# A low-rank update on one core: x's column blocks taken with a step of six, and A and B loaded behind the first piece of x

## The chip, the cores and the metric

The kernel runs on one core of one Trainium2 chip. A time is the device time of one execution in microseconds (us). Beside it stand the numbers of one profiled execution: its span runs from the first to the last instruction that the hardware profiler recorded, and some time lies around it. TensorE is PE in the profile (PEld is its weight load, which can run beside a matmul), VectorE is DVE, ScalarE is ACT, GpSimd is POOL, SyncE is SP. A small q behind a name (SPq, ACTq) is that engine's instruction sequencer, which also issues DMAs.

## What is computed

```python
batch, seq, d_model, r = 16, 512, 768, 16
# x [16, 512, 768] float32, A [768, 16], B [16, 768], scale 0.5
lora = np.matmul(np.matmul(x, A), B)
return (x + scale * lora).astype(np.float32)
```

With the first two axes of x flattened there are 8192 rows (tokens) of 768 float32. x is 25.17 MB, the output is as large, and A and B are 48 KB each.

## The kernel before

**Loads and stores.** The 8192 tokens are cut into six parts, `PARTS = [2, 6, 8, 16, 16, 16]`, in units of 128 tokens. Part i is loaded by one DMA into a tile of 128 partitions by S rows of 768 float32, S being its entry in the list; partition p gets S neighbouring tokens, so each partition's piece is one contiguous run of S times 3072 bytes. All x loads and all stores are issued by SyncE and so share one DMA queue (q1 in the profile) in the order in which they are issued: the loads of parts 0 to 4 (line 68), the load of part 5 (line 96), and then the stores (line 155) as parts are finished. Parts 0 to 3 are each stored in one DMA, parts 4 and 5 in two halves of eight rows (3.1 MB each). The result is written over x in place (line 145), so a part needs no second buffer.

**A and B.** TensorE multiplies over the partitions, so A's 768 rows must come to lie as six blocks of 128 partitions. Column block j of x is its columns 128j to 128j+127, and block j of A is the rows with these numbers. A row of A is only 16 float32, or 64 bytes. So A is loaded as 24 runs of 2048 bytes, 32 rows of A each (line 79, issued by ScalarE on its own queue, q10), into a corner of the room that part 5 will take later. GpSimd has cleared that corner first (line 78). VectorE then transposes it in blocks of 32 by 32 (line 87) and four casts (line 91) put the result into `a_mm`, float16, [128, 6, 16]. B is loaded by ScalarE as well (line 80) and cast to float16 (line 93). Because part 5's tile is the same memory as this corner, its load waits until VectorE has read A and B from there.

**The work on x.** The 64 row blocks are handled in 17 chunks of up to four. For each chunk:
- `transposed`: for each of six column blocks j, TensorE transposes the chunk's 128x128 float32 blocks into PSUM (line 113; up to four transposes), and ScalarE copies the result to SBUF as float16 (line 115). In a transpose the block of x is the stationary operand, loaded by LDWEIGHTS, and the identity matrix moves past it.
- `projected`: six matmuls, one for each j, add up (x A) transposed, 16 by 512 (line 122); VectorE multiplies by the scale and casts (line 127).
- `added`: for each 128 tokens two matmuls of 512 and 256 columns with B (line 139), and VectorE adds the result to x (line 145).
- `finished`: issues a store when its last chunk is added (line 155).

**Order.** The loop at the end of the kernel interleaves the chunks: half of chunk c's transposes, half of chunk c-1's `added`, the rest of the transposes, the rest of `added`, then `projected`. The framework's scheduler may move an instruction when its own estimate of the times says that another can go first, and it did so around the first parts. Each engine then works through its own instructions in order; semaphores carry the dependences.

Of the kernel before, what the change touches and what calls it, by code (L numbers as in the profile page):

```python
# [1 line left out]

# [6 lines left out]


MM_DT = mybir.dt.float16

PARTS = [2, 6, 8, 16, 16, 16]

STORES = {4: [8, 8], 5: [8, 8]}

CHUNK = 4


@with_exitstack  # L20
def kernel(
    ctx: ExitStack,
    tc: tile.TileContext,
    x: bass.AP,
    A: bass.AP,
    B: bass.AP,
    scale: bass.AP,
    out: bass.AP,
):

    nc = tc.nc
    fp32 = mybir.dt.float32
    P = 128

    x2 = x.flatten_outer_dims()
    out2 = out.flatten_outer_dims()
    T, D = x2.shape
    R = A.shape[1]  # L40
    ND = D // P
    assert D % P == 0 and sum(PARTS) * P == T
    n_splits = [(n0, min(512, D - n0)) for n0 in range(0, D, 512)]
    sc = float(scale)

    const = ctx.enter_context(tc.tile_pool(name="const", bufs=1))
    xpool = ctx.enter_context(tc.tile_pool(name="xp", bufs=1))
    xtpool = ctx.enter_context(tc.tile_pool(name="xtp", bufs=6))
    ypool = ctx.enter_context(tc.tile_pool(name="yp", bufs=2))
    ps_xt = ctx.enter_context(tc.tile_pool(name="ps_xt", bufs=3, space=bass.MemoryType.PSUM))  # L50
    ps_y = ctx.enter_context(tc.tile_pool(name="ps_y", bufs=1, space=bass.MemoryType.PSUM))
    ps_l = ctx.enter_context(tc.tile_pool(name="ps_l", bufs=2, space=bass.MemoryType.PSUM))


    parts = []
    tok = 0
    for i, S in enumerate(PARTS):
        parts.append([None, tok, S])
        tok += S * P

    def rows(t2, i):
        _, tok0, S = parts[i]
        return t2[ds(tok0, S * P), :].rearrange("(p s) d -> p s d", s=S)

    def loaded(i):
        S = parts[i][2]
        parts[i][0] = xpool.tile([P, S, D], fp32, name=f"x_sb{i}")
        nc.sync.dma_start(out=parts[i][0], in_=rows(x2, i))  # L68


    last = len(parts) - 1
    lastpool = ctx.enter_context(tc.tile_pool(name="lastp", bufs=1))
    room = lastpool.tile([P, parts[last][2], D], fp32, name="room", tag="last")
    NB = D // 32
    a_rows = room[0:32, 0, 0 : 32 * R].rearrange("b (a r) -> b a r", r=R)
    a_t = room[0:32, 1, 0 : 32 * R].rearrange("a (r b) -> a r b", r=R)
    b_f32 = room[0:R, 2, :]
    nc.gpsimd.memset(a_rows, 0.0)  # L78
    nc.scalar.dma_start(out=a_rows[0:NB, :, :], in_=A.rearrange("(b a) r -> b a r", a=32))
    nc.scalar.dma_start(out=b_f32, in_=B)  # L80
    loaded(0)
    loaded(1)
    for i in range(2, last):
        loaded(i)


    nc.vector.transpose(out=a_t, in_=a_rows.rearrange("b a r -> b r a"))  # L87
    a_mm = const.tile([P, ND, R], MM_DT, name="a_mm")
    a_tv = a_t[:, :, 0:NB].rearrange("a r (c k) -> a k c r", k=4)
    for k in range(4):  # L90
        nc.vector.tensor_copy(out=a_mm[ds(32 * k, 32), :, :], in_=a_tv[:, k, :, :])  # L91
    b_mm = const.tile([R, D], MM_DT, name="b_mm")
    nc.vector.tensor_copy(out=b_mm, in_=b_f32)  # L93

    parts[last][0] = lastpool.tile([P, parts[last][2], D], fp32, name="x_last", tag="last")
    nc.sync.dma_start(out=parts[last][0], in_=rows(x2, last))

    ident = const.tile([P, P], fp32, name="ident")
    make_identity(nc, ident)


    chunks = [
        (i, s0, min(CHUNK, S - s0))
        for i, (_, _, S) in enumerate(parts)
        for s0 in range(0, S, CHUNK)
    ]
    state = {}

    def transposed(c, j):
        i, s0, n = chunks[c]  # L110
        xt_ps = ps_xt.tile([P, CHUNK, P], fp32, name="xt_ps")
        for s in range(n):
            nc.tensor.transpose(xt_ps[:, s, :], parts[i][0][:, s0 + s, ds(j * P, P)], ident)  # L113
        xt_sb = xtpool.tile([P, CHUNK * P], MM_DT, name="xt_sb")
        nc.scalar.copy(out=xt_sb[:, 0 : n * P], in_=xt_ps[:, 0:n, :])  # L115
        state[c, j] = xt_sb

    def projected(c):
        n = chunks[c][2] * P
        ps_yt = ps_y.tile([R, CHUNK * P], fp32, name="ps_yt")  # L120
        for j in range(ND):
            nc.tensor.matmul(  # L122
                ps_yt[:, 0:n], a_mm[:, j, :], state.pop((c, j))[:, 0:n],
                start=(j == 0), stop=(j == ND - 1),
            )
        yt_sb = ypool.tile([R, CHUNK * P], MM_DT, name="yt_sb")
        nc.vector.tensor_scalar(  # L127
            out=yt_sb[:, 0:n], in0=ps_yt[:, 0:n], scalar1=sc, scalar2=None,
            op0=mybir.AluOpType.mult,
        )  # L130
        state[c] = yt_sb

    def added(c, subs):
        i, s0, n = chunks[c]
        subs = [s for s in subs if s < n]
        lora = {s: ps_l.tile([P, D], fp32, name="lora_ps") for s in subs}
        for s in subs:
            for n0, w in n_splits:
                nc.tensor.matmul(  # L139
                    lora[s][:, ds(n0, w)], state[c][:, ds(s * P, P)], b_mm[:, ds(n0, w)],  # L140
                    start=True, stop=True,
                )
        for s in subs:
            xs = parts[i][0][:, s0 + s, :]
            nc.vector.tensor_tensor(out=xs, in0=xs, in1=lora[s], op=mybir.AluOpType.add)  # L145

    def finished(c):
        i, s0, n = chunks[c]
        del state[c]
        end = 0  # L150
        for w in STORES.get(i, [parts[i][2]]):
            end += w
            if end == s0 + n:
                piece = slice(end - w, end)
                nc.sync.dma_start(out=rows(out2, i)[:, piece, :], in_=parts[i][0][:, piece, :])

    for c in range(len(chunks)):
        for j in range(3):
            transposed(c, j)
        if c >= 1:  # L160
            added(c - 1, (0, 1))
        for j in range(3, ND):
            transposed(c, j)
        if c >= 1:
            added(c - 1, (2, 3))
            finished(c - 1)
        projected(c)
    c = len(chunks) - 1
    added(c, (0, 1))
    added(c, (2, 3))  # L170
    finished(c)


# [1 line left out]
_INS = ['x', 'A', 'B', 'scale']  # L175
_OUTS = [((16, 512, 768), 'float32')]

_NUMBERS = {'scale': 0.5}


# [26 lines left out]
```

## Time and profile before

| | |
|---|---|
| time, median of 3 runs | 124.87 us (124.79 to 125.25) |
| the profiled execution: its own time | 124.9 us |
| the profiled execution: its span | 123.1 us |
| PE busy (matmuls and transposes) | 97.8 us, 79% |
| DVE busy | 70.3 us, 57% |
| ACT busy | 52.5 us, 43% |
| bytes moved by DMA | 50.54 MB, mean 410 GB/s over the span |
| first x load issued, landed | 0.74 us, 6.1 us |
| second x load landed; PE's next transpose | 11.6 us; 11.76 us |
| last x load landed | 64.1 us |
| last store issued, landed | 110.46 us, 122.3 us |

Busy time counts an engine's own instructions. Idle time on an engine that is not the bound costs nothing, and a busy share near 80% does not make an engine the bound: what matters is which wait ends last. The windows of the profile give, for a stretch of the span, each engine's busy time, the granted TensorE clock, the share of the 16 DMA engines' time that is filled with packets, and the rate.

### The profile page before, as it was taken

To read this page: it belongs to the slowest core of one execution; us is meant where nothing else is said; L and a number is where in the kernel's file an instruction comes from. 1 tells how busy PE (TensorE), PEld (TensorE's weight loads), DVE (VectorE), ACT (ScalarE), POOL (GpSimd) and SP (SyncE) were. 2 spreads that over 40 slices of the span, in tenths; PEclk is the share of its full clock that TensorE was granted. 3 is DMA by queue.
4 is the path that set the end of the run, shared out by engine and by line. 5 is a ranking of instruction groups with operands and counts; after the bars stand their busy time and mean duration, and the time that the engine had idled before them with its cause. 6 is when DMAs were issued, how large, how long until landed. Compare 5 with 4: busy or idle time off the path is not lost.

```text
span 123.1 us, 1615 instructions
## 1 busy us (share of the span) xinstructions
PE 97.8 (79%) x614; PEld 60.8 (49%) x614; DVE 70.3 (57%) x87; ACT 52.5 (43%) x103; POOL 1.1 (1%) x7
## 2 busy tenths in 40 slices
PE   0095999999949999999999999999999999530000
PEld 0083765657328566656657474757565666100000
DVE  0261056755884276868686868685767768880000
ACT  3060556455406573645555564737373736000000
POOL 3000000000000000000000000000000000000000
PEclk9999999999999999999999999999999999995555
DMA  2999998999799699799799999989979999999981
GB/s 61 406 431 427 471 519 367 415 500 431 335 511 479 290 511 468 319 479 495 295 411 462 444 407 495 479 351 479 452 311 463 415 439 426 421 447 439 415 383 64
DMA packets 2092, 50.54 MB, mean 410 GB/s; under 512 B 252, under 2 KB 252, under 8 KB 548
## 3 DMA queue, kind: packets, MB, share of 16 engines
q1 hardware_dynamic: 2016, 50.33, 95.6%
q10 hardware_dynamic: 68, 0.10, 0.4%
q8 instruction: 5, 0.08, 0.3%
q14 instruction: 3, 0.02, 0.0%
HBM read 25.26 MB, written 25.17 MB: 410 GB/s over the span
## 4 chain that ended last, share of the span: by engine, by line
PE 71%; DMA 8%; DVE 7%; issue 1%; DVEq 1%; SPq 0%; ACT 0%; ACTq 0%
PE xt_ps L113 38%; PE lora_ps L139 18%; PE ps_yt L122 15%; DMA x_sb<-in_x_dram 8%; DVE x_last L145 3%; DVE x_sb L145 3%; DVE yt_sb L127 1%; DVEq L202 1%; SPq L68 0%; ACT xt_sb L115 0%; ACTq L115 0%
## 5 line engine op out<-in xcount | busy, mean ns | idle before, releaser
L115 ACT CAST xt_sb<-xt_ps 128x512 f16<-128x512 f32 (+1 forms) x102 | 51.2, 569 | 49.9 <-PE xt_ps L113 49.6
L145 DVE TENSOR_TENSOR x_sb<-x_sb,lora_ps 128x768 f32<-128x768 f32 x48 | 43.5, 950 | 21.2 <-PE lora_ps L139 21.2
L113 PE MATMUL xt_ps<-ident,x_sb 128*128 128x128 f32 x288 | 39.7, 290 | 7.7 <-DMA x_sb<-in_x_dram 7.6
L113 PEld LDWEIGHTS xt_ps<-ident,x_sb 128*128 128x128 f32 x288 | 33.1, 147 | 16.7 <-issue 11.5
L139 PE MATMUL lora_ps<-b_mm,yt_sb 16*128 16x512 f16 (+1 forms) x128 | 26.8, 324 | 3.8 <-DVE yt_sb L127 1.6
L122 PE MATMUL ps_yt<-xt_sb,a_mm 128*16 128x512 f16 (+1 forms) x102 | 24.4, 375 | 0.0
L145 DVE TENSOR_TENSOR x_last<-x_last,lora_ps 128x768 f32<-128x768 f32 x16 | 14.5, 950 | 5.3 <-PE lora_ps L139 5.3
L139 PEld LDWEIGHTS <-yt_sb 16*128 16x128 f16 x128 | 9.5, 92 | 15.3 <-issue 8.3
L127 DVE TENSOR_SCALAR yt_sb<-ps_yt 16x512 f16<-16x512 f32 (+1 forms) x17 | 10.9, 642 | 7.9 <-PE ps_yt L122 7.9
L122 PEld LDWEIGHTS <-a_mm 128*16 128x16 f16 x102 | 7.9, 91 | 13.0 <-issue 5.1
L113 PE MATMUL xt_ps<-ident,x_last 128*128 128x128 f32 x96 | 12.2, 277 | 0.0
L113 PEld LDWEIGHTS xt_ps<-ident,x_last 128*128 128x128 f32 x96 | 10.3, 140 | 3.0 <-PE ps_yt L122 1.7
L93 DVE CAST b_mm<-room 16x768 f16<-16x768 f32 x1 | 0.5, 548 | 4.4 <-DMA room<-in_B_dram 4.4
L115 ACT ACT_TABLE_LOAD x1 | 1.3, 1283 | 1.9 <-POOL ident masks.py:199 1.9
L87 DVE STREAM_TRANSPOSE room<-room 32x512 f32<-32x512 f32 x1 | 1.0, 1031 | 1.1 <-DMA room<-in_A_dram 1.1
L91 DVE CAST a_mm<-room 32x96 f16<-32x96 f32 x4 | 0.9, 232 | 0.1
L78 POOL MEMSET room<- 32x512 f32 x1 | 0.5, 515 | 0.3 <-POOLq L188 0.3
masks.py:199 POOL TENSOR_SCALAR_AFFINE_SELECT ident<-ident 128x128 f32<-128x128 f32 x1 | 0.3, 292 | 0.1
masks.py:197 POOL MEMSET ident<- 128x128 f32 x1 | 0.2, 194 | 0.0
L188 POOL MEMSET const-bfloat16-1.0<- 128x1 bf16 x1 | 0.1, 101 | 0.0
L188 POOL MEMSET const-uint8-127<- 128x1 uint8 x1 | 0.1, 101 | 0.0
L188 POOL MEMSET const-float32-0.0<- 128x1 f32 x1 | 0.1, 98 | 0.2 <-issue 0.2
(1 smaller groups left out, 0.1 us busy)
## 6 DMA issues: line engine op xcount, KB each, us to landing
x_sb<-in_x_dram SPq DMA_DIRECT2D x2, 6144.0 KB, 39.7
out_dram<-x_sb SPq DMA_DIRECT2D x3, 3072.0 KB, 21.6
x_last<-in_x_dram SPq DMA_DIRECT2D x1, 6144.0 KB, 56.0
out_dram<-x_sb SPq DMA_DIRECT2D x1, 6144.0 KB, 28.2
out_dram<-x_last SPq DMA_DIRECT2D x2, 3072.0 KB, 13.5
x_sb<-in_x_dram SPq DMA_DIRECT2D x1, 3072.0 KB, 17.3
x_sb<-in_x_dram SPq DMA_DIRECT2D x1, 2304.0 KB, 10.5
out_dram<-x_sb SPq DMA_DIRECT2D x1, 2304.0 KB, 44.6
```

What stands on the lines that cost most here:

```text
L78: nc.gpsimd.memset(a_rows, 0.0)
L87: nc.vector.transpose(out=a_t, in_=a_rows.rearrange("b a r -> b r a"))
L91: nc.vector.tensor_copy(out=a_mm[ds(32 * k, 32), :, :], in_=a_tv[:, k, :, :])
L93: nc.vector.tensor_copy(out=b_mm, in_=b_f32)
L113: nc.tensor.transpose(xt_ps[:, s, :], parts[i][0][:, s0 + s, ds(j * P, P)], ident)
L115: nc.scalar.copy(out=xt_sb[:, 0 : n * P], in_=xt_ps[:, 0:n, :])
L122: nc.tensor.matmul(ps_yt[:, 0:n], a_mm[:, j, :], state.pop((c, j))[:, 0:n], start=(j == 0), stop=(j == ND - 1),)
L127: nc.vector.tensor_scalar(out=yt_sb[:, 0:n], in0=ps_yt[:, 0:n], scalar1=sc, scalar2=None, op0=mybir.AluOpType.mult,)
L139: nc.tensor.matmul(lora[s][:, ds(n0, w)], state[c][:, ds(s * P, P)], b_mm[:, ds(n0, w)], start=True, stop=True,)
L145: nc.vector.tensor_tensor(out=xs, in0=xs, in1=lora[s], op=mybir.AluOpType.add)
L188: nc = _bacc.Bacc("TRN2", target_bir_lowering=False, num_devices=1)
L202: with _tile.TileContext(nc) as tc:
```

## The change

A's rows are split the other way: partition k gets the six rows 6k to 6k+5, which are one contiguous run of 384 bytes, so A is one plain load of 128 such runs into `a_f32` and one cast to `a_mm`. The clearing, the 32x32 transpose and three of the four casts are gone. For the product to stay the same, column block j of x becomes the columns j, j+6, j+12, ...: a transpose now reads 128 float32 that lie 24 bytes apart in each partition, where before it read 128 neighbouring ones. The sum over the six blocks covers all 768 columns either way.

A and B are issued by SyncE, on x's queue, directly behind the load of part 0 and ahead of the load of part 1. They have tiles of their own, so part 5 takes an ordinary tile and its load is issued right behind that of part 4, with no wait.

```diff
-    last = len(parts) - 1
-    lastpool = ctx.enter_context(tc.tile_pool(name="lastp", bufs=1))
-    room = lastpool.tile([P, parts[last][2], D], fp32, name="room", tag="last")
-    NB = D // 32
-    a_rows = room[0:32, 0, 0 : 32 * R].rearrange("b (a r) -> b a r", r=R)
-    a_t = room[0:32, 1, 0 : 32 * R].rearrange("a (r b) -> a r b", r=R)
-    b_f32 = room[0:R, 2, :]
-    nc.gpsimd.memset(a_rows, 0.0)
-    nc.scalar.dma_start(out=a_rows[0:NB, :, :], in_=A.rearrange("(b a) r -> b a r", a=32))
-    nc.scalar.dma_start(out=b_f32, in_=B)
+    a_f32 = const.tile([P, ND, R], fp32, name="a_f32")
+    b_f32 = ypool.tile([R, D], fp32, name="b_f32", bufs=1)
     loaded(0)
-    loaded(1)
-    for i in range(2, last):
+    nc.sync.dma_start(out=a_f32, in_=A.rearrange("(k j) r -> k j r", j=ND))
+    nc.sync.dma_start(out=b_f32, in_=B)
+    for i in range(1, len(parts)):
         loaded(i)
-    nc.vector.transpose(out=a_t, in_=a_rows.rearrange("b a r -> b r a"))
     a_mm = const.tile([P, ND, R], MM_DT, name="a_mm")
-    a_tv = a_t[:, :, 0:NB].rearrange("a r (c k) -> a k c r", k=4)
-    for k in range(4):
-        nc.vector.tensor_copy(out=a_mm[ds(32 * k, 32), :, :], in_=a_tv[:, k, :, :])
+    nc.vector.tensor_copy(out=a_mm, in_=a_f32)
     b_mm = const.tile([R, D], MM_DT, name="b_mm")
     nc.vector.tensor_copy(out=b_mm, in_=b_f32)
-    parts[last][0] = lastpool.tile([P, parts[last][2], D], fp32, name="x_last", tag="last")
-    nc.sync.dma_start(out=parts[last][0], in_=rows(x2, last))
...
+    def xt_in(i, s, j):
+        return parts[i][0][:, s, :].rearrange("p (k j) -> p j k", j=ND)[:, j, :]
...
-            nc.tensor.transpose(xt_ps[:, s, :], parts[i][0][:, s0 + s, ds(j * P, P)], ident)
+            nc.tensor.transpose(xt_ps[:, s, :], xt_in(i, s0 + s, j), ident)
```

## The prediction

> **What bounds the kernel now.** I first read the page's table of 40 slices and its queue list.
>
> ```profile
> PE   0095999999949999999999999999999999530000
> PEclk9999999999999999999999999999999999995555
> DMA  2999998999799699799799999989979999999981
> ...
> q1 hardware_dynamic: 2016, 50.33, 95.6%
> q10 hardware_dynamic: 68, 0.10, 0.4%
> ```
>
> Two rows are dense: PE stops near slice 36, the DMA engines go on to the end. The windows settle which one ends last; the columns are the stretch, busy time and count of each engine, granted clock, share of the 16 DMA engines, GB/s.
>
> ```profile
> 1.80:2.40 0.60, 0.00 (x0) 0.00 (x0) 0.00 (x0) 0.55 (x1) 0.00 (x0) 1.00 0.78 169
> 2.40:3.00 0.60, 0.00 (x0) 0.00 (x0) 0.00 (x0) 0.60 (x1) 0.00 (x0) 1.00 0.57 102
> 3.00:64.10 61.10, 54.54 (x338) 34.64 (x339) 35.68 (x47) 29.43 (x61) 0.00 (x0) 1.00 1.00 428
> 64.10:110.46 46.36, 43.25 (x278) 26.19 (x276) 34.63 (x42) 21.89 (x42) 0.00 (x0) 1.00 1.01 431
> 110.46:112.80 2.34, 0.00 (x0) 0.00 (x0) 0.00 (x0) 0.00 (x0) 0.00 (x0) 0.50 1.05 452
> 112.80:119.50 6.70, 0.00 (x0) 0.00 (x0) 0.00 (x0) 0.00 (x0) 0.00 (x0) 0.50 1.00 429
> 119.50:122.30 2.80, 0.00 (x0) 0.00 (x0) 0.00 (x0) 0.00 (x0) 0.00 (x0) 0.50 0.23 97
> ```
>
> From 3.0 to 119.5 us the DMA engines are full, at about 430 GB/s. The kernel is bound by its 50 MB; computing only has to hand over each store before the queue is empty. The tightest place is the last store, issued at 110.46. The three last rows move 1.06 + 2.87 + 0.27 = 4.2 MB after that; the store itself is 3.15 MB, so 1.05 MB is still ahead of it: 2.45 us at 430 GB/s. A store issued into an empty queue would start about 1.1 us after its issue (the first load: issued at 0.74, first bytes at about 1.8). So **PE and what follows it may be 2.45 - 1.1 = 1.35 us later at no cost**; beyond that each us costs about one. This cover is small, because PE never rests: the chain of waits runs through PE from the landing of part 1 to the end.
>
> ```profile
> 11.76 2.79 PE xt_ps L113 x12
> ...
> 40.23 1.39 PE ps_yt L122 x6
> 41.62 1.46 PE xt_ps L113 x12
> 43.08 0.75 PE lora_ps L139 x4
> 43.83 1.46 PE xt_ps L113 x12
> ```
>
> No DMA wait stands in it after 11.76, so whatever makes a transpose slower accumulates from there.
>
> **The transposes, the part with the largest possible price.** 384 of them now load a stationary block whose elements lie 24 bytes apart. What a load has to spare is in narrow stretches of the timeline and in the groups by shape (start or busy us, mean ns).
>
> ```profile
> 70.62 0.20 PEld L113 LDWEIGHTS xt_ps<-ident,x_sb 128*128 128x128 f32 x2 [0.43 <-PE ps_yt L122]
> ```
> ```profile
> 70.78 0.25 PEld L113 LDWEIGHTS xt_ps<-ident,x_sb 128*128 128x128 f32 x2
> ```
> ```profile
> L113 PEld LDWEIGHTS xt_ps<-ident,x_last 128*128 128x128 f32 x96 | 10.3, 140 | 3.0 <-PE ps_yt L122 1.7 <-issue 1.3
> L122 PEld LDWEIGHTS <-a_mm 128*16 128x16 f16 x102 | 7.9, 91 | 13.0 <-issue 5.1
> L91 DVE CAST a_mm<-room 32x96 f16<-32x96 f32 x4 | 0.9, 232 | 0.1
> ```
>
> One load record is 140 ns. The first two of a run of twelve together take 200, so the second starts 60 ns after the first: a load reads its 128 columns in about 60 ns. (The record of a load of 16 columns is 91 ns; 112 columns more make 49, which agrees.) Later pairs take 250, so they start 110 ns apart: inside a run the pace is set by the transposing matmul, and the load lies under it with about 50 ns to spare. The first load of a run has no cover; between the runs PE changes to other matmuls.
>
> No row shows PE reading with a step, so I bound the new load from both sides. Below: 60 ns, nothing changes (less is excluded, as the same 128 columns are read). Above: the cast into a_mm reads on VectorE, each of its 96 elements 128 bytes from the last. The scale-and-cast takes 409 ns for 256 columns and 673 for 512, so 1.03 ns each and 145 fixed; 96 at that pace make 244, and the cast took 232. So a step costs VectorE nothing, and a new place in every 1.03 ns is reached. If PE could do no better, a load would take 128 x 1.03 + 5 = 137 ns. Between 60 and 137 I take the middle, about 100: neither row is PE with a step. That is still under the 110. Then only the first load of each run shows: two runs for each of 16 chunks after part 1's landing, 32 x 40 ns = **1.3 us**, just the cover of 1.35. At 137 ns: 32 x 77 = 2.5 us, and the 340 others pass the cover by 27 ns, 9.2 us; together 11.7.
>
> [...]
>
> **A, B and the queue.** The profile gives A and B's queue (q10) 0.4% of 16 engines' span: 0.49 us of every engine. Afterwards there are 128 + 16 pieces in place of 24 + 16. Below: by bytes alone 98 KB at 430 GB/s is 0.23 us, a gain of 0.26. Above: if a piece of A's takes as long as q10's average packet (0.49 x 16 / 68 = 0.115 us), 144 x 0.115 / 16 = 1.04 us, a loss of 0.55. I take 0.5, no change, since bytes fall short of a small piece's fixed part and the average packet is far larger than 384 bytes.
>
> [...]
>
> At the start, 1.8 to 3.0 us moved 101 + 61 = 163 KB where the full rate makes 514: 0.8 us lost, while part 0 and B share the engines. With B behind part 0, between nothing and 0.8 comes back. I take 0.1, because a queue that starts up alone also has to fill. On SyncE two issues, 0.54 and 0.41 us as ScalarE's took, now stand ahead of part 1's: it is issued at about 2.1 instead of 1.17 and could start at 3.2. Part 0's 0.79 MB last until 1.8 + 1.8 = 3.6, so it is not late. If that cover were gone it would cost the difference, as PE waits for part 1. Part 5's load, issued at 8.17 now, comes earlier behind 19 MB of queue, which hides its issue time either way: it lands at 64.1 and PE needs it at about 80. The stores are issued from 17 us on, and no wait is added.
>
> **What goes from the prologue**: the 0.52 us clearing on GpSimd, the 1.03 us transpose and three casts of 0.23 on VectorE. a_mm is now ready at 8.1 us and first used at 8.97, behind chunk 0's transposes; afterwards A lands soon after part 0. PE then waits for part 1 until 11.76 anyway, idle 1.34 us, so these gains go into that wait. If A came later than now, the same 1.34 us would hide it.
>
> **Sum**, from this execution's span of 123.1 and 1.8 us around it (124.9; the median is 124.87): transposes +1.3, less 1.35 of cover, and about 0.3 because the 16 engines do not come free at one moment and some would wait; A and B 0; start -0.1. That is +0.2: **125.1 us**, with 124.3 to 125.5 as this case's own range.
>
> **Rivals.**
> - *The load overtakes its cover* (slower). Place: line 113's pace. Price: above about 100 to 110 ns the cover is used up, and from 110 on each further ns costs 372 ns in all. At 115 ns: 32 x 55 + 340 x 5 = 3.5 us, less 1.35: 127.0. At 137: 11.7 less 1.35: 135.3. For it: every element is at a new place, and cover and middle value are near each other. Against: the cast on VectorE. The lower half is likelier, since PE's own load of neighbouring columns reads twice as fast as VectorE.
> - *Several times longer* (slower). A load of 230 ns, about four times: 32 x 170 + 340 x 120 = 46 us, less 1.35: near 170. Nothing in the trace excludes it, the cast's row speaks against it.
> - *Faster by over 0.5%.* The load stays near 60 ns, and the start gives back most of its 0.8 with A's pieces cheap (-0.26): 123.8 to 124.2. For it: the slow 1.2 us at the start. Against: the bytes are the same and 116 of 123 us are full.
> - *The short pieces do not pay*: A's pieces at the upper bound, +0.55, with the load hidden: 125.4 to 125.6. I count it in the forecast's edge.
>
> **How the numbers follow.** Forecast 46%; load overtakes 32%, two thirds of that below 131; several times longer 12%; faster 10%. 0.5% is 0.62 us, about what a measurement of this kernel can tell from no change. Faster by more: 0.10. Within: 0.45, the forecast less its upper edge and a little of the first rival. Slower: 0.45. The range runs from 124.0 into the first rival up to 131.0; beyond it lie the rest of that rival and the second.
>
> **What will show it.** Right: loads of line 113 recorded at about 180 instead of 140 ns; transposes still 110 ns apart; twelve in about 1.5 us; the last store issued near 111.8; DMA full to about 119.5. Wrong: a run of twelve well over 1.5 us, a last store issued after 112, empty DMA slices ahead of it; or loads still at 140 and the start fuller, then the gain of the third rival. An early order of PE's work changed by the scheduler would move the last store too, by an amount that this trace cannot give.

## The result, and the profile after

The changed kernel takes 133.76 us (median of 6 runs) against 124.88 before; the ratio is 1.0697, with a 95% interval of 1.0666 to 1.0728. (One of the six runs, of 135.2 us, fell into a slower state of the chip and is left out of the ratio.) The forecast of 125.1 us was wrong, and so was the range up to 131.0: the first rival came true near its upper end. The profiled execution took 133.08 us with a span of 131.3, 8.2 us longer than before.

The same rows of the page as before:

```profile
PE   0384999999769999999999999999999999973000
PEclk9997699999995999999999999999999999999555
DMA  4999999999999999998999999998999922890885
...
q1 hardware_dynamic: 2192, 50.43, 90.7%
```

PE is still dense up to slice 36 or 37, of a longer span now. What is new stands in the DMA row: slices 33 and 34 hold a 2, and slice 37 a 0. Windows of the changed kernel (stretch, busy time of each engine, granted clock, DMA share, GB/s) show these holes in us:

```profile
64.90:105.00 40.10, 40.10 (x236) 27.55 (x236) 25.70 (x31) 20.50 (x37) 0.00 (x0) 1.00 1.01 432
105.00:111.60 6.60, 6.60 (x41) 4.51 (x40) 4.23 (x5) 3.41 (x7) 0.00 (x0) 1.00 0.28 119
111.60:118.50 6.90, 6.11 (x35) 3.51 (x34) 4.52 (x6) 2.93 (x6) 0.00 (x0) 1.00 0.95 400
118.50:122.60 4.10, 0.96 (x4) 0.27 (x3) 3.25 (x4) 0.00 (x0) 0.00 (x0) 0.80 0.02 4
122.60:130.50 7.90, 0.00 (x0) 0.00 (x0) 0.00 (x0) 0.00 (x0) 0.00 (x0) 0.50 0.93 398
```

Up to 105 us the queue is full, as before. Then it runs dry twice, because the last two stores are not issued yet. PE, busy without a gap up to 116.9 us, has become the bound of the last 25 us; the last store is issued at 121.78 us, 11.3 later than before. The chain of waits shows where PE's time went (start, us, what):

```profile
44.88 1.82 PE xt_ps L101 x12
46.70 0.75 PE lora_ps L127 x4
47.45 1.83 PE xt_ps L101 x12
49.28 0.75 PE lora_ps L127 x4
50.03 1.39 PE ps_yt L110 x6
```

The matmuls with A and B take 1.39 and 0.75 us as before. Only a run of twelve transposes is longer, 1.82 where it was 1.46. A chunk has two, so it takes 6.54 us in place of 5.81; 16 chunks of 0.73 make 11.7, and 11.3 were measured. That the two are so near is partly luck. From the fourth store to the last both kernels run at the full granted clock, and the seven chunks whose transposes lie there lose 5.13 us, 0.73 each, as they should. Between the third store and the fourth, four chunks lose 4.65 us in place of 2.9; there the granted clock stood at half from 39.1 to 42.5 us in this execution, and not in that of the kernel before. Up to the third store only 1.54 us are lost.

Inside a run, in narrow stretches of the timeline of the weight loads (start, busy us), and over all loads (mean ns):

```profile
70.99 0.35 PEld L101 LDWEIGHTS xt_ps<-ident,x_sb 128*128 128x128 f32 x2 [0.43 <-PE ps_yt L110]
```
```profile
71.23 0.38 PEld L101 LDWEIGHTS xt_ps<-ident,x_sb 128*128 128x128 f32 x2
```
```profile
L101 PEld LDWEIGHTS xt_ps<-ident,x_sb 128*128 128x128 f32 x384 | 57.5, 236 | 18.3 <-issue 8.1 <-PE ps_yt L110 5.6 <-ACT xt_sb L103 4.6
L79 DVE CAST a_mm<-a_f 128x96 f16<-128x96 f32 x1 | 0.2, 211 | 5.3 <-DMA a_f<-in_A_dram 5.3
```

A record is about 240 ns now. The first two loads of a run cover 350, so the second starts 110 ns after the first (60 before; single records say 107 and 57). Two later ones cover 380, so they start 140 ns apart (110 before; single records say 134 to 137 and 109). So a load that reads every sixth column takes 107 ns at the head of a run and 137 in a stream, and there it passes its cover.

### The profile page after: what moved, and what is told of

Same layout as the page of the kernel before. It is cut to its first block, busy times and chain, and to the rows that moved or that the text cites. A ratio compares the mean times of both kernels' runs of the same rounds, so it can differ in the third digit from the quotient of the medians.

```text
span 131.3 us, 1607 instructions
## 1 busy us (share of the span) xinstructions
PE 109.1 (83%) x614; PEld 74.7 (57%) x614; DVE 68.6 (52%) x83; ACT 55.9 (43%) x103; POOL 0.7 (1%) x6
## 4 chain that ended last, share of the span: by engine, by line
PE 75%; DMA 8%; DVE 6%; issue 1%; SPq 1%; DVEq 1%
PE xt_ps L101 45%; PE lora_ps L127 16%; PE ps_yt L110 14%; DMA x_sb<-in_x_dram 8%; DVE x_sb L133 5%; DVE yt_sb L115 1%; DVEq L190 1%; SPq L75 0%; SPq L74 0%; SPq L68 0%
## 5 line engine op out<-in xcount | busy, mean ns | idle before, releaser
L103 ACT CAST xt_sb<-xt_ps 128x512 f16<-128x512 f32 (+1 forms) x102 | 54.7, 561 | 58.8 <-PE xt_ps L101 58.3
L133 DVE TENSOR_TENSOR x_sb<-x_sb,lora_ps 128x768 f32<-128x768 f32 x64 | 58.0, 951 | 31.9 <-PE lora_ps L127 31.8
L101 PE MATMUL xt_ps<-ident,x_sb 128*128 128x128 f32 x384 | 63.7, 320 | 7.1 <-DMA x_sb<-in_x_dram 7.1
L101 PEld LDWEIGHTS xt_ps<-ident,x_sb 128*128 128x128 f32 x384 | 57.5, 236 | 18.3 <-issue 8.1
L110 PE MATMUL ps_yt<-xt_sb,a_mm 128*16 128x512 f16 (+1 forms) x102 | 23.9, 369 | 0.0
L81 DVE CAST b_mm<-b_f 16x768 f16<-16x768 f32 x1 | 0.5, 549 | 1.1 <-DMA b_f<-in_B_dram 1.1
```

What stands on the lines that cost most here:

```text
L101: nc.tensor.transpose(xt_ps[:, s, :], xt_in(i, s0 + s, j), ident)
L110: nc.tensor.matmul(ps_yt[:, 0:n], a_mm[:, j, :], state.pop((c, j))[:, 0:n], start=(j == 0), stop=(j == ND - 1),)
```

## The experiments

Times are medians; "before" was 124.97 us beside these runs. PE's pitch is the distance between two transposes inside a run, at the full granted clock.

**The two halves of the change, and the other operand.** The prologue alone:

```diff
-        return parts[i][0][:, s, :].rearrange("p (k j) -> p j k", j=ND)[:, j, :]
+        return parts[i][0][:, s, ds(j * P, P)]
```

> The changed kernel with blocks of 128 neighbouring columns of x again; A stays loaded as 128 runs of 384 bytes, so block j of x meets other rows of A than the reference's. Theory P (the step of 24 bytes in the transposes makes all of the 8.9 us): the last store is issued at about 110.5 us again, time 124.6 to 125.2. Theory Q (A and B in x's queue cost something too): part 5 landed at 64.9 us in the changed kernel against 64.1, so the full DMA queue ends about 0.8 us later, time 125.5 to 125.9. The pitch of the transposes is 109 to 110 ns under both.

Measured: 125.73 us, ratio 1.0077 (1.0031 to 1.0123); pitch 109 ns; last store issued at 111.1. Theory P, that the step makes all of it, is not quite right: the prologue costs something, but it is a small share. The time is that of theory Q, but its way isn't shown: part 5 landed at 64.14 us here, and at 64.12 in the kernel before.

The step alone, put into the kernel before:

```diff
+    def xt_in(i, s, j):
+        return parts[i][0][:, s, :].rearrange("p (k j) -> p j k", j=ND)[:, j, :]
...
-            nc.tensor.transpose(xt_ps[:, s, :], parts[i][0][:, s0 + s, ds(j * P, P)], ident)
+            nc.tensor.transpose(xt_ps[:, s, :], xt_in(i, s0 + s, j), ident)
```

> The kernel before, with only its transposes reading every sixth column; A's layout is left as it was, so block j of x meets other rows of A than the reference's. Theory P: all of the change's loss, 133.3 to 134.2 us, pitch 137 ns inside a run of twelve, last store issued at about 121.5. Theory Q does not say otherwise for this one: once PE sets the end, a queue that is 0.8 us later is hidden, so 133 to 134 as well; a time below 132.5 would say that the prologue shares the 8.9 us.

Measured: ratio 1.0728 (1.0665 to 1.0792), 133.53 us in the profiled execution, pitch 136 ns, last store issued at 122.1. The step alone has the whole loss of the change: the change's interval lies inside this one. What the prologue costs does not add to it, since by then PE sets the end. Its run of twelve in the chain of waits:

```profile
64.87 1.83 PE xt_ps L116 x12
```

Why a load takes 107 ns alone and 137 in a stream was open. The first idea was that PE reads the loaded block and the moving identity over one path (theory S, an estimate of the author's: 107 ns for 128 columns are 0.83 ns each, and 27 ns more, up to 134, are 32 times that). It was tried with the step in the identity alone, as below, and with this edit and the one above together:

```diff
-    ident = const.tile([P, P], fp32, name="ident")
-    make_identity(nc, ident)
+    ident_c = const.tile([P, P], fp32, name="ident_c")
+    make_identity(nc, ident_c)
+    ident_w = const.tile([P, P, 6], fp32, name="ident_w")
+    ident = ident_w[:, :, 0]
+    nc.gpsimd.tensor_copy(out=ident, in_=ident_c)
```

> The kernel before, with the identity matrix kept in columns 24 bytes apart; x is read in neighbouring columns as before, and GpSimd makes one more copy at the start. Theory S (PE reads the block that it loads and the operand that moves over one path, which takes a new place every 0.83 ns, 107 ns for 128 columns; four neighbouring float32 count as one place): 128 + 32 places, as in the changed kernel, only with the parts exchanged, so the pitch is about 137 ns again and the time about 133 us. Theory L (the load has its own path and simply takes 134 ns once a matmul runs beside it): the identity is the moving operand and has 107 ns for its 128 columns, so the pitch stays 109 ns and the time 124.9 us, up to 126 if the longer start shows.

> The kernel before with both steps: transposes that read every sixth column of x, and the identity in columns 24 bytes apart; block j of x meets other rows of A than the reference's. Theory S: 128 + 128 places of 0.83 ns, a pitch of about 216 ns, so 372 x 0.107 = 40 us more than before less the cover, about 163 us. Theory L: the load's 134 ns set the pitch at 137, and the time is that of the changed kernel, about 133.5 us.

Measured: 182.69 us, ratio 1.4611 (1.4578 to 1.4643), with the step in the identity alone, and 183.12 in a single run with both. Both theories fall. The pitch is about 230 ns in both kernels, against 137 and 109 (theories S and L) for the first, 216 and 137 for the second. The chains of the two kernels, one line each:

```profile
66.02 2.94 PE xt_ps L116 x12
```
```profile
65.18 2.96 PE xt_ps L119 x12
```

A step in the moving operand alone doubles a transpose (230 ns against 109), and a step in the loaded block then adds almost nothing (2.96 us for the run of twelve, against 2.94): its load, 134 to 137 ns in a stream, is shorter than that pitch. So the two don't share one path that simply adds their reads, and a step costs far more on the operand that moves (a pitch of 230 ns) than on the one that is loaded (136).

**Smaller steps, and less that moves.** Each is the changed kernel with another slice, here the step of two (the step of four has a 4 in both places):

```diff
-        return parts[i][0][:, s, :].rearrange("p (k j) -> p j k", j=ND)[:, j, :]
+        return parts[i][0][:, s, j : j + 127 * 2 + 1 : 2]
```

> The changed kernel with blocks of every second column (8 bytes apart; six overlapping blocks that start at columns 0 to 5, so it is not the reference's product). [...] Theory N (any step makes every element cost 0.83 ns): second load after 107 ns, pitch 136, about 133.5 us.

> The same with every fourth column (16 bytes apart), not the reference's product. [...] Theory N: the same. A cost that grows with the distance between elements would lie in between, a pitch of 120 to 130 ns and 128 to 132 us.

Measured in a single run each: 129.68 us with a pitch of 119 ns (step of two, 8 bytes), and 128.3 us with 121 ns (step of four, 16 bytes). The second load starts 97 ns after the first in both, where it was 57 with neighbouring columns and 107 with a step of six. So not every step costs the same, as theory N had it (107 ns, and a pitch of 136), and from 8 to 16 bytes the load grows no longer. What sets its time is not shown. One chain line of each kernel, the step of two first:

```profile
64.08 1.63 PE xt_ps L101 x12
```
```profile
62.38 1.64 PE xt_ps L101 x12
```

With steps of two and of four the run of twelve takes 1.63 and 1.64 us, with a step of six 1.82. (That the step of four has the shorter total goes with the start of the two executions, in which part 1 landed at 12.69 and 11.86 us, and with the granted clock, which stood at half from 37.2 to 44.1 and from 39.3 to 42.7 us.)

With half the identity, each transpose made as two (the second kernel has the slice of neighbouring columns besides):

```diff
-            nc.tensor.transpose(xt_ps[:, s, :], xt_in(i, s0 + s, j), ident)
+            for h in range(2):
+                nc.tensor.transpose(
+                    xt_ps[:, s, ds(64 * h, 64)], xt_in(i, s0 + s, j)[0:64, :], ident[0:64, 0:64]
+                )
```

> The changed kernel with each transpose made as two, each loading 128 columns, 24 bytes apart, of the first 64 partitions, and moving only 64 columns of the identity past them; both halves come from the same rows, so it is not the reference's product, and there are 768 transposes in place of 384. The matmul itself then needs half as long (53 ns), so the load alone sets the pitch. Theory I (in the change the identity's own reading takes 27 ns from the load, in proportion to its 128 columns): 107 + 14, a pitch of about 121 ns. Theory K (27 ns pass after each load whatever moves): 134 to 136 ns. If the reading does not interfere when less moves: 107 ns. All three are far slower in total than the change, about 372 more transposes of 105 to 136 ns, so 170 to 185 us.

> The half-identity kernel once more, now with blocks of 128 neighbouring columns: 768 transposes, each loading 128 columns of the first 64 partitions and moving 64 columns of the identity; not the reference's product. Where the granted clock is full the matmul needs 53 ns, so the load sets the pitch and shows what one costs in a steady stream without a step. Theory K (some 27 ns pass with every load beyond the first of a run, with or without a step): 57 + 27 = 84 ns, so the cover in the kernel before was 25 ns and not 50. Theory D (only a load with a step is drawn out, 107 alone and 134 in a stream): 57 to 60 ns. At half the clock the matmul needs 107 ns and hides either.

Measured, in a single run each: 216.62 us with the step, beyond the 170 to 185 expected, since the granted clock was at half for most of the span and the other matmuls were slow too (those of 512 columns 427 ns apart, 216 at the full clock); 190.01 us with neighbouring columns. At the full clock the pitch is 133 to 137 ns with the step and 62 to 64 without; at half it is 135 and 107. (The profile's clock reads full until its first record, at 41.0 and 83.3 us in these two, but the matmuls of 512 columns are 427 ns apart there too, so it counts as half here.) The stretches in which each kernel had it, first with the step and then without:

```profile
92.20:95.50 3.30, 3.30 (x25) 2.92 (x24) 0.16 (x2) 1.62 (x3) 0.00 (x0) 1.00 0.00 0
```
```profile
83.30:86.60 3.30, 3.30 (x44) 2.74 (x42) 1.82 (x2) 2.48 (x5) 0.00 (x0) 1.00 0.02 5
```

25 matmuls against 44 in 3.3 us. So a load in a stream takes 63 ns without a step: the 60 of the prediction, and its cover of 50, were right. With the step it takes about 135 whether 64 or 128 columns of the identity move (theory K, against I). The 27 ns on top of 107 belong to the stepped load itself in a stream (theory D for the load without a step). They are the same at half the granted clock, so they don't follow the pace of the matmuls. What they are isn't settled. Both kernels load 64 partitions and the change 128; with the step the pitch at the full clock is about 136 ns in both cases.

**Could the idea be saved with a step of three?** That a load with a shorter step would stay under the matmul's 109 ns was the author's estimate; no run before had shown it. A is read as 256 runs of 192 bytes, and A and B stay on ScalarE's queue:

```diff
-    nc.sync.dma_start(out=a_f32, in_=A.rearrange("(k j) r -> k j r", j=ND))
-    nc.sync.dma_start(out=b_f32, in_=B)
+    nc.scalar.dma_start(out=a_f32.rearrange("k (g h) r -> k g h r", g=2), in_=A.rearrange("(g k h) r -> k g h r", g=2, h=3))
+    nc.scalar.dma_start(out=b_f32, in_=B)
...
-        return parts[i][0][:, s, :].rearrange("p (k j) -> p j k", j=ND)[:, j, :]
+        return parts[i][0][:, s, :].rearrange("p (g k h) -> p g h k", g=2, h=3)[:, j // 3, j % 3, :]
```

> The reference's product with a step of three: columns 0 to 383 and 384 to 767 are cut into three interleaved blocks each, 12 bytes between a block's columns, so A is read as 256 runs of 192 bytes and still needs one cast; A and B are issued by ScalarE on its own queue as in the kernel before. [...] Theory N: pitch 136 ns, about 133 us.

Measured: ratio 1.0175 (1.0094 to 1.0257), 128.05 us in the profiled execution. The pitch is 114 ns, and not the 136 of theory N; the load at the head of a run takes 95. A run of twelve:

```profile
63.66 1.56 PE xt_ps L101 x12
```

0.10 us more than before, 32 times, is 3.2 us; the last store is issued at 116.77, 6.3 later than before. The rest probably comes from the granted clock, which was at half from 13.0 to 19.8 us and again from 40.3 to 43.7; every transpose takes 213 ns then. The stores agree: from the fourth to the last, at the full clock, only 1.5 us are lost in seven chunks, 0.21 each, which is the longer runs alone; the other 4.8 are lost before. The clock was not tested by itself. The step of three is dearer than the kernel before.

**What the prologue costs.** A's short pieces and their place in the queue, one without the other: the prologue alone (the slice of neighbouring columns), with A and B issued by ScalarE; and the kernel before, with its old 2048-byte runs issued by SyncE.

```diff
-    nc.sync.dma_start(out=a_f32, in_=A.rearrange("(k j) r -> k j r", j=ND))
-    nc.sync.dma_start(out=b_f32, in_=B)
+    nc.scalar.dma_start(out=a_f32, in_=A.rearrange("(k j) r -> k j r", j=ND))
+    nc.scalar.dma_start(out=b_f32, in_=B)
```

> The changed kernel with neighbouring columns, as in the prologue alone, but A's 128 runs of 384 bytes and B are issued by ScalarE on its own queue again; block j of x meets other rows of A than the reference's. If the place in x's queue made the prologue's +0.3 to +0.8 us (the rate from 4 to 5 us fell to 224 GB/s there), the time is that of before, 124.7 to 125.2, and 4 to 5 us is above 400 GB/s. If the short pieces made it, or the other early order of PE's work, it stays at 125.4 to 126.

```diff
-    nc.scalar.dma_start(out=a_rows[0:NB, :, :], in_=A.rearrange("(b a) r -> b a r", a=32))
-    nc.scalar.dma_start(out=b_f32, in_=B)
     loaded(0)
+    nc.sync.dma_start(out=a_rows[0:NB, :, :], in_=A.rearrange("(b a) r -> b a r", a=32))
+    nc.sync.dma_start(out=b_f32, in_=B)
```

> The kernel before with one edit: A's 24 runs of 2048 bytes and B are issued by SyncE behind the load of part 0, with the old layout work. If the place in x's queue costs: 125.3 to 125.8 us, with a rate near 220 GB/s from 4 to 5 us and near 300 from 1.8 to 3. If the short pieces cost: 124.7 to 125.1.

Measured: 125.08 us, ratio 1.0005 (0.9991 to 1.0019), for the pieces; 125.72 us, ratio 1.0052 (1.0035 to 1.0069), for the place. So 128 pieces of 384 bytes and the layout work that they spare, taken together, make no difference that can be measured; the place costs about 0.65 us. From 1.8 to 3 and from 4 to 5 us, in the kernel before, with the pieces on ScalarE's queue, and with the place alone:

```profile
1.80:3.00 1.20, 0.00 (x0) 0.00 (x0) 0.00 (x0) 1.15 (x1) 0.00 (x0) 1.00 0.67 136
...
4.00:5.00 1.00, 0.00 (x0) 0.00 (x0) 0.55 (x1) 0.00 (x0) 0.00 (x0) 1.00 1.54 547
```
```profile
1.80:3.00 1.20, 0.00 (x0) 0.00 (x0) 0.00 (x0) 1.14 (x1) 0.00 (x0) 1.00 0.63 172
...
4.00:5.00 1.00, 0.00 (x0) 0.00 (x0) 0.00 (x0) 0.00 (x0) 0.00 (x0) 1.00 1.24 490
```
```profile
1.80:3.00 1.20, 0.00 (x0) 0.00 (x0) 0.00 (x0) 0.21 (x1) 0.00 (x0) 1.00 0.81 287
...
4.00:5.00 1.00, 0.00 (x0) 0.00 (x0) 0.01 (x1) 0.00 (x0) 0.00 (x0) 1.00 1.05 316
```

Part 0 alone at the head of the queue does start faster (287 against 136 GB/s), but behind A and B the rate drops (316 against 547 from 4 to 5 us), and part 1 lands at 12.5 us in place of 11.6. PE then starts later, in another order of work, as the scheduler had it. But at the third store it is level again (issued at 38.51 us, and at 38.50 in the kernel before). That its last store is issued at 113.2, 2.75 later, comes after that: 2.62 of it lie between the third and the fourth store, where the granted clock stood at half from 36.1 to 42.9 us in this execution. (The prologue alone loses 2.53 us between these two stores, with the clock at half from 33.8 to 40.6.) 2.75 is less than the cover of 3.1 worked out below, so PE's delay need not show in the time. The loads don't wait for PE, and the last of them landed 0.65 later (64.77 against 64.12). So in this execution the loss stands in the queue; but in the prologue alone, with A and B in the same place, the last load landed at 64.14, so how the place costs isn't settled.

**An attempt to beat both**: A and B issued later by ScalarE, so that part 0 has the queue to itself.

```diff
+    ident = const.tile([P, P], fp32, name="ident")
+    make_identity(nc, ident)
+    nc.scalar.copy(out=a_rows[0:1, 0, 0:1], in_=ident[0:1, 0:1])
+    nc.scalar.copy(out=b_f32[0:1, 0:1], in_=ident[0:1, 0:1])
     nc.scalar.dma_start(out=a_rows[0:NB, :, :], in_=A.rearrange("(b a) r -> b a r", a=32))
     nc.scalar.dma_start(out=b_f32, in_=B)
...
-    ident = const.tile([P, P], fp32, name="ident")
-    make_identity(nc, ident)
```

> An attempt to beat both: the kernel before with neighbouring columns, but ScalarE issues A and B only after two copies of one element that wait for the identity matrix, so at about 3.3 us; part 0 then has the DMA engines to itself. From 1.8 to 3 us the rate should be near 290 GB/s as in the prologue alone (136 before: 0.19 MB, 0.43 us at 430 GB/s) with no fall behind it, since part 1 is issued at 1.2 us as before. Then 124.4 to 124.7 us. If B and A cost the engines the same wherever they come, 124.9.

Measured: ratio 1.0224 (1.0171 to 1.0278). The attempt failed by its own hand, as the order at the start of its timeline shows:

```profile
2.13 0.19 ACT L82 COPY room<-ident 1x1 f32<-1x1 f32 x1
...
6.07 0.37 ACT L116 CAST xt_sb<-xt_ps 128x256 f16<-128x256 f32 x1 [3.76 <-PE xt_ps L114]
6.08 0.61 ACTq L83 DMA_DIRECT2D room<-in_A_dram  x1
6.73 0.33 ACTq L84 DMA_DIRECT2D room<-in_B_dram  x1
```

The scheduler placed the two issues behind ScalarE's first copy out of PSUM, which waits for PE. A was issued at 6.08 us instead of 3.3 and landed at 13.6, and PE waited for it until 15.7. Whether an issue at 3.3 would gain the expected 0.3 us was not tried.

## Why the prediction was wrong, point by point

- **The bound and its cover: right in kind, too small in size.** The DMA engines did bound the kernel before, and the hand-over of the last store is where the change bites. But the cover was taken as 1.35 us. The last store is now issued 11.3 us later and the span is 8.2 longer, so it was 3.1. The stores show it: with an empty queue the last one lands 8.7 us after its issue (121.78 to 130.46 here; 8.68 to 8.69 in the kernels with a step alone, of two, of three and of four), and before it took 11.83. The 1.35 came from the queue's bytes and so was a mean over the 16 DMA engines. At the old end they finished raggedly, from 119.5 to 122.3 at 97 GB/s. By the packets of each engine, the first came to the last store at 112.4 us and the last at 114.7, and those that began it last finished last; they had the most cover. Behind the empty queue all began it between 122.6 and 122.75.
- **The load: the step that failed.** "Between 60 and 137 I take the middle, about 100: neither row is PE with a step." The load measured 107 ns at the head of a run and 134 to 137 in a stream, the upper bound. The first figure alone would, by the prediction's own sum, have left the forecast standing (107 is under 109); what was missing is that a stepped load in a stream is longer than one by itself, which no row before could show. The 60 ns without a step and the 50 ns of cover held (63 in a stream). So did the reading of the cast on VectorE: 96 elements without a step took 211 ns in the changed kernel, 232 with a step of 128 bytes before. It was no row of PE, and PE's load with a step takes about twice that without (107 against 57 ns at the head of a run, 135 against 63 in a stream).
- **The first rival's sum was right.** At 137 ns it had 11.7 us on PE; 11.3 were measured, partly by luck, as said above, but 0.73 us in each chunk at the full clock. It said 135.3 us and 133.08 came in the profiled execution, the difference being mainly the cover. Its place, line 113's pace, was the right one, and its chance of 32% with the upper third outside the range was the mistake in weighing: a value in the middle was preferred to the only row that shows reading with a step.
- **The start: wrong in sign, small.** Part 1 was to be "not late". It landed at 12.05 us in place of 11.62, and the prologue alone costs 0.8% (0.3 to 1.2%). Its own part 1 landed at 11.74, though, so a late part 1 doesn't explain that cost, which stays open. The gain from 1.8 to 3 us came as foreseen (246 and 379 GB/s) and was given back at once behind it (238 from 4 to 5 us).
- **A's pieces and the layout work: right, taken together.** No change was taken between -0.26 and +0.55 us for the pieces, and none for the layout work, which went into PE's wait for part 1; the two together measured 1.0005. In the packets the short pieces are the slower ones: 384 bytes took 22 ns on their engine, and 24576 bytes of a store 0.91 us, so 17 against 27 GB/s. In the kernel's time no price of that shows.

## What to carry to other kernels

A step in an operand that TensorE reads is not free because VectorE reads one almost for free (here 232 ns with a step and 211 without, while PE's load went from 57 to 107). Find what each weight load has to spare under its matmul, and count a stepped load in a stream at twice its time, as here (63 to 135 ns with float32 and a step of six). On the moving side the step cost more still (a pitch of 230 ns and not 136). Work out what the saved prologue was hidden under before paying for it on every instruction of the steady state: here nothing was gained there, and 0.36 us was paid 32 times. When a full queue hides a late store, measure the cover at the DMA engine that finishes last, and not at the mean (here 3.1 us and not 1.35).

## What the runs showed of the hardware, unexpected

- A load of 128 float32 columns, of which the second starts after (head of a run) and the pitch in a run: neighbouring 57 and 109 ns; step of two 97 and 119; of three 95 and 114; of four 97 and 121; of six 107 and 136. It does not rise evenly with the distance, and the reason stays open.
- The identity with a step of six, as the moving operand: a pitch of 230 ns, 2.1 times that of a plain one (227 at half the clock, where a plain one has 213), and with a step in both operands no more than that.
- At half the granted clock a transpose takes 213 ns with and without a step in the loaded block, longer than either load (63 and 135 ns in a stream). The stepped load itself doesn't follow the clock: where only 64 columns of the identity move, the pitch is 135 ns at half the clock and 133 to 137 at the full one.
- In the changed kernel the clock stood at half from 39.1 to 42.5 us, shortly after PE had waited three times for VectorE (0.79, 0.72 and 0.38 us, from 35.2 to 38.3). The kernel before has the same three waits, from 33.6 to 36.8, and kept the full clock. So the waits alone don't set it, and what does is open.
- The profile's clock reads full until its first record. In the kernel before that comes at 14.8 us, and the transposes ahead of it are 213 ns apart, as at half.
